# Sums read behind later splits in an expert stage, and one weight chunk in eight of some blocks multiplied without a split

## The chip, the cores and the metric

The kernel runs on one core of a Trainium2 chip. The metric is the device time of one execution in microseconds (us). Five engines take part: PE (TensorE, matrix products), DVE (VectorE), ACT (ScalarE), POOL (GpSimd, hardly used here) and SP (SyncE, which issues the loads). Each works through its own queue of instructions in order; semaphores make one wait for another. PE writes its sums into PSUM, eight banks of 128 partitions x 512 floats.

## The reference

Two transformer-like blocks over 256 tokens of width 1024, all in float32. The last and longest part is a mixture of eight experts of which each token uses two:

```
logits = h @ router_w + router_b
top_val, top_idx = top_k(logits, 2);  top_w = softmax(top_val)
for e in range(8):
    out += gates[:, e] * ((silu(h @ wg[e]) * (h @ wu[e])) @ wd[e])
```

`wg` and `wu` are 1024 x 3584, `wd` is 3584 x 1024, so the experts' weights are 352 MB, and each is read once.

## The kernel before

**Products.** A float32 product is made of three fast ones: each operand is split into a high half (rounded to the fast type fp32r) and a low half (the rest), and `mm3` adds high x high, high x low and low x high into the same bank. A split (`split`, lines 373 to 376) is a cast on ACT (line 374) and a subtraction on DVE (recorded under line 339, which `tt` uses). A plain float32 product needs no split; PE's records show it as two matmul records for one.

**Weights.** A chunk is 512 rows x 512 columns (1 MiB), laid out in memory so that one load fetches it; `raw` and `fetch` (line 393) take a raw buffer and issue the load on SP's queue. `chunk` splits it in two steps of 128 x 1024 elements into buffers `hi` and `lo`. In the expert stage there are eight raw buffers (ten at first) and six `hi` and six `lo` buffers, that is, three chunks. A buffer is free again when its last reader is done: a raw one after the second subtraction, a split one after its matmuls. Buffers are given out in the order in which they came free.

**The expert stage** (`moe`). The experts are ordered by the number of their tokens. The four largest get 128 slots each, the four others (`small`) 64. `gather` collects an expert's tokens into slots by products with a selection matrix and splits them (`XH`, `XL`); for 64 slots the high and low halves share the 128 columns, so two products do for three. An expert has seven blocks (`cb`) of 512 hidden columns. A block is six chunks:

- `up`: gate chunks 0 and 4, then up chunks 0 and 4 (numbers are the first of the four 128-row tiles), summed into one bank each;
- the gate sum goes through Silu, the product with the up sum is transposed on PE and split (`hu`);
- `down`: two chunks, which add into two banks that stay for the whole expert.

**Order.** The blocks of the 128-slot experts and those of the 64-slot experts run in turn, after four 128-slot blocks at the start and before four 64-slot ones at the end. The work is written as a pipeline: after `up` of a block come `down` half 0 of the block before, `up_end` of this block, and `down` half 1 of the block before. `mids` holds four lists of work that is run behind the four chunks of the next `up`: `end` (the split of `hu`) in the first, gathers, scatters and placements of experts in the others. A scheduler orders each engine's queue from this program order and from when it reckons an operand ready; `tc.issue_after(ins)` puts what is traced in its block behind `ins` on the same engine. `last_hi` and `last_lo` are the latest cast and subtraction of a split.

Readers of sums before: Silu of the gate sum directly behind the gate chunks; for 64 slots, copies of the gate sum (line 2128) and of the up sum (line 2138), and Silu and product only after the transposes, in `end`; the multiply of the 128-slot block in `up_end`; the `hu` cast (line 2160) and its subtraction in `end`. PSUM has three banks of class `pd` and five of class `ps` here; four `ps` hold the down sums of two experts.

At the end the last block's `end` and the last two down chunks' splits come ahead of a branch (`overflow`, for experts with too many tokens; not taken with these inputs), and the last `down`, the scatter, the norm and the stores behind it.

Of the kernel before, what the change touches and what calls it, by code (L numbers as in the profile page):

```python
# [212 lines left out]
class K:  # L213
# [1784 lines left out]
            self.nc.scalar.copy(PG, p[:, :256])  # L1998


    def gather(self, x, P, a2, b2, out, part=(0, 4)):
        for k0 in part:
            with self.scope():
                p, f = self.psum(), self.med()
# [49 lines left out]
    def moe(self, x, lg, rs):  # L2054
        A, nc = self.A, self.nc
        ad = self.ada_b
# [12 lines left out]
        NE, NB = 8, 7  # L2069
        small = [r >= SMALL for r in SEQ]  # L2070
# [21 lines left out]
        def begin(e):  # L2092
            P, PG = PP[e % 4]
            if small[e]:
                X = self.take("r", 0)
                state[e] = [PG, (X,), None]
                return [lambda: self.gather_small(x, P, ad["a2"], ad["b2"], X)]
            XH, XL = self.take("r", 0), self.take("r", 0)
            state[e] = [PG, (XH, XL), None]
            out = lambda k0, f: self.split(f, XH[:, k0 * 128 : k0 * 128 + 512], XL[:, k0 * 128 : k0 * 128 + 512])  # L2100
            return [lambda k0=k0: self.gather(x, P, ad["a2"], ad["b2"], out, (k0,)) for k0 in (0, 4)]

        def up(e, cb, mids):
            XH, XL = state[e][1][0], state[e][1][-1]
            g, ps = self.med(), []
            for nm in ("moe_w_gate_2", "moe_w_up_2"):
                p = self.take("pd")
                ps.append(p)  # L2110
                for kh in (0, 4):
                    with self.scope():
                        args = (W(nm, e), kh * 128, 4, cb * 512, 512)
                        c = self.chunk(*args)
                        for k in range(4):
                            ks = slice((kh + k) * 128, (kh + k) * 128 + 128)
                            if small[e]:
                                for i in range(2):
                                    self.last_mm = self.mm(p, XH[:, ks], c[k][i], kh + k + i == 0, kh + k + i == 8, True)
                            else:  # L2120
                                self.mm3(p, XH[:, ks], XL[:, ks], c[k][0], c[k][1], kh + k == 0, kh + k == 7)
                    for f in mids.pop(0):
                        f()
                if not small[e] and nm == "moe_w_gate_2":
                    self.act(g, p, AF.Silu)
            if small[e]:
                with self.tc.issue_after(self.last_hi.ins):
                    nc.scalar.copy(g, ps[0])
            return g, p


        def up_end(e, g, pu):
            hu = self.take("r", 0)
            p = self.take("ps", 0)
            if small[e]:
                gu = self.med()
                with self.tc.issue_after(self.last_hi.ins):
                    nc.scalar.copy(gu, pu)  # L2138
                for i, a in enumerate((g, gu)):
# [3 lines left out]
                def end():  # L2143
                    with self.scope():
                        h = self.med()
                        self.act(h[:, :256], p[:, :256], AF.Silu)
                        self.tt(h[:, 256:], p[:, 256:], h[:, :256], ALU.mult)
                        v = hu[:, :512].rearrange("p (k h s) -> p k h s", k=4, h=2)
                        self.split(h[:, 256:].rearrange("p (k s) -> p k s", k=4), v[:, :, 0], v[:, :, 1])
                    self.free(p)  # L2150
                return hu, end
            with self.scope():
                h = self.med()
                self.tt(h, pu, g, ALU.mult)
                for k in range(4):
                    self.tr(p[:, k * 128 : k * 128 + 128], h[:, k * 128 : k * 128 + 128])

            def end():
                with self.tc.issue_after(self.last_hi.ins):
                    self.last_hi = nc.scalar.copy(hu[:, :512], p)  # L2160
                with self.tc.issue_after(self.last_lo.ins):
                    self.tt(hu[:, 512:], p, hu[:, :512].bitcast(F32), ALU.subtract)
                self.free(p)
            return hu, end

        def down(e, cb, hu, half):
            hh, hl = hu[:, :512], hu[:, 512:]
            if cb == half == 0:
                state[e][2] = [self.take("ps", 0), self.take("ps", 0)]
            acc = state[e][2]  # L2170
            with self.scope():
                c = self.chunk(W("moe_w_down_2", e), cb * 512, 4, half * 512, 512)
                for k in range(4):
                    ks = slice(k * 128, k * 128 + 128)
                    first, last = cb == 0 and k == 0, cb == NB - 1 and k == 3
# [3 lines left out]
                    else:  # L2179
                        self.mm3(acc[half], hh[:, ks], hl[:, ks], c[k][0], c[k][1], first, last)  # L2180
            if half:
                self.free(hu)
# [18 lines left out]
        prev, mids = None, [[] for _ in range(4)]  # L2201
        for e, cb in steps:
            with self.scope():
                gp = up(e, cb, mids)
                mids = [[] for _ in range(4)]
                if cb == NB - 1:
                    self.free(*state[e][1])
                if prev:
                    down(*prev, 0)
                hu, end = up_end(e, *gp)  # L2210
                mids[0].append(end)
            if prev:
                for i, f in zip((1, 2), down(*prev, 1) or []):
                    mids[i].append(f)
            prev = (e, cb, hu)
# [97 lines left out]
```

## Time and profile before

| what | value |
|---|---|
| time, median of 3 runs (lowest, highest) | 2152.31 us (2149.79, 2153.07) |
| profiled execution: its time, its span | 2151.22 us, 2149.4 us |
| PE busy, share of the span | 2066.2 us, 96% |
| DVE busy | 1841.5 us, 86% |
| ACT busy | 1325.3 us, 62% |
| loads of the experts' weights | 336 of 1024 KB |
| data moved, mean rate | 610.70 MB, 284 GB/s |
| mean granted TensorE clock | 0.988 of 2.4 GHz |

The span runs from the first to the last instruction. Busy PE includes matmuls that wait in its pipeline. The expert stage is about 1165 to 2130 us of the span.

### The profile page before, as it was taken

How to read it: one execution, taken by the hardware profiler on the slowest of the kernel's cores; microseconds unless marked ns; L12 is line 12 of the kernel's file. 1: busy time of each engine (PE TensorE's matmuls, PEld its weight loads, DVE VectorE, ACT ScalarE, POOL GpSimd, SP SyncE). 2: the span in 40 equal slices, each digit the busy share in tenths (PEclk: the TensorE clock that was granted, in tenths of full speed). 3: DMA queues.
4: the chain of work that ended last, by engine and by line, in shares of the span. 5: the costliest groups of instructions: out<-in, count | busy, mean ns of one | idle time of the engine just before them, and what ended most of it. 6: DMA issues, size and time to landing. Idle time of an engine off the chain costs nothing. (4 is left out here: it accounts for less than half of the span.)

```text
span 2149.4 us, 31135 instructions
## 1 busy us (share of the span) xinstructions
PE 2066.2 (96%) x11593; PEld 1706.1 (79%) x11593; DVE 1841.5 (86%) x2669; ACT 1325.3 (62%) x1857; POOL 2.1 (0%) x6
## 2 busy tenths in 40 slices
PE   6999999999999999999999999999999999999997
PEld 5987888889988878998997887777777777777765
DVE  6888985898888868888787999998998899998997
ACT  4544354454445435444765887777787778777775
POOL 0000000000000000000000000000000000000000
PEclk9999999999999999999999999999999999999997
DMA  7546767878843527885465899998999899998993
GB/s 306 192 165 214 264 219 255 298 296 303 302 160 117 150 100 262 310 342 212 139 253 188 329 400 368 356 387 321 391 343 377 348 365 377 355 383 322 386 371 140
DMA packets 99997, 610.70 MB, mean 284 GB/s; under 512 B 19156, under 2 KB 24061, under 8 KB 27773
## 3 DMA queue, kind: packets, MB, share of 16 engines
q1 hardware_dynamic: 99836, 608.64, 75.7%
q8 instruction: 92, 1.51, 0.3%
q14 instruction: 69, 0.56, 0.1%
HBM read 606.75 MB, written 3.42 MB: 284 GB/s over the span
## 5 line engine op out<-in xcount | busy, mean ns | idle before, releaser
L354 PE MATMUL pd<-k 128*128 128x512 f32 (+2 forms) x7408 | 1447.2, 349 | 37.8 <-DVE k L339 26.6
L339 DVE TENSOR_TENSOR k<-k,k 128x1024 fp32r<-128x1024 f32 (+2 forms) x1149 | 1229.8, 1112 | 184.4 <-ACT k L374 180.9
L354 PEld LDWEIGHTS pd<-k 128*128 128x128 f32 (+1 forms) x7408 | 1139.1, 190 | 269.3 <-DVE k L339 104.0
L374 ACT CAST k<-k 128x1024 fp32r<-128x1024 f32 (+2 forms) x1131 | 1039.6, 977 | 362.9 <-PE pd L354 184.6
L354 PE MATMUL ps<-k 128*128 128x512 f32 (+8 forms) x3031 | 576.2, 343 | 13.4 <-DVE k L339 3.8
L354 PEld LDWEIGHTS ps<-k 128*128 128x128 f32 (+4 forms) x3031 | 431.6, 179 | 112.1 <-DVE k L339 18.2
L348 DVE SCALAR_TENSOR_TENSOR k<-k,k 128x512 f32<-128x512 f32 (+1 forms) x257 | 188.3, 735 | 2.1 <-ACT k L351 0.2
L351 ACT ACTIVATE k<-pd 128x256 f32<-128x256 f32 (+1 forms) x125 | 57.2, 481 | 101.4 <-PE pd L354 98.5
L351 ACT ACTIVATE k<-k 128x256 f32<-128x256 f32 (+8 forms) x142 | 69.0, 500 | 79.3 <-DVE k L339 41.7
L339 DVE TENSOR_TENSOR k<-k 128x512 f32<-128x512 f32 (+13 forms) x277 | 93.6, 355 | 17.3 <-ACT k L351 12.4
L354 PEld LDWEIGHTS ps<-k,k 128*128 128x128 f32 x526 | 77.0, 199 | 12.4 <-DVE k L348 3.4
L339 DVE TENSOR_TENSOR k<-ps,k 128x512 fp32r<-128x512 f32 (+5 forms) x99 | 56.8, 579 | 24.8 <-PE ps L354 8.7
L354 PE MATMUL ps<-k,k 128*128 128x64 f32 (+3 forms) x526 | 75.0, 269 | 2.9 <-DVE k L348 2.9
L357 PE MATMUL ps<-k,k 128*128 128x128 f32 (+1 forms) x396 | 60.8, 278 | 16.7 <-DVE k L343 15.8
L357 PEld LDWEIGHTS ps<-k,k 128*128 128x128 f32 (+1 forms) x396 | 47.9, 143 | 30.5 <-DVE k L343 18.5
L339 DVE TENSOR_TENSOR k<-pd,k 128x512 f32<-128x512 f32 (+4 forms) x108 | 59.8, 568 | 12.5 <-PE pd L354 6.5
L351 ACT ACTIVATE k<-ps,k 128x128 f32<-128x128 f32 (+2 forms) x100 | 36.6, 446 | 42.8 <-DVE k L348 26.7
L348 DVE SCALAR_TENSOR_TENSOR k<-pd,k,k 128x255 f32<-128x255 f32 (+2 forms) x96 | 43.1, 474 | 4.4 <-ACT k L351 4.0
L2138 ACT COPY k<-pd 128x512 f32<-128x512 f32 x28 | 16.4, 586 | 48.2 <-PE pd L354 47.9
L345 DVE TENSOR_SCALAR k<-ps,k 128x128 f32<-128x128 f32 (+1 forms) x90 | 32.4, 405 | 10.5 <-PE ps L354 6.9
L348 DVE SCALAR_TENSOR_TENSOR k<-k 128x256 f32<-128x256 f32 (+7 forms) x121 | 36.9, 312 | 2.8 <-ACT k L351 1.1
L351 ACT ACTIVATE k<-ps 128x256 f32<-128x256 f32 (+2 forms) x30 | 12.4, 420 | 35.3 <-PE ps L354 35.3
(95 smaller groups left out, 416.1 us busy)
## 6 DMA issues: line engine op xcount, KB each, us to landing
k<-in_moe_w_up_dram SPq DMA_DIRECT2D x112, 1024.0 KB, 7.0
k<-in_moe_w_gate_dram SPq DMA_DIRECT2D x112, 1024.0 KB, 7.1
k<-in_moe_w_down_dram SPq DMA_DIRECT2D x112, 1024.0 KB, 7.2
k<-in_ada_w_dram SPq DMA_DIRECT2D x48, 1024.0 KB, 5.3
k<-in_w_in_dram SPq DMA_DIRECT2D x44, 1024.0 KB, 6.1
k<-in_w_ff_dram SPq DMA_DIRECT2D x32, 1024.0 KB, 6.0
k<-in_w_ada_dram SPq DMA_DIRECT2D x24, 1024.0 KB, 6.7
k<-in_cd_w_in_dram SPq DMA_DIRECT2D x14, 1024.0 KB, 4.9
```

The lines of the kernel that those rows point to most:

```text
L339: return self.nc.vector.tensor_tensor(o, a, b, op=op)
L345: self.nc.vector.tensor_scalar(o, a, s1, s2, op0=op0, op1=op1)
L348: self.nc.vector.scalar_tensor_tensor(o, a, s, b, op0=op0, op1=op1)
L351: return self.nc.scalar.activation(o, a, f, **kw)
L354: return self.nc.tensor.matmul(o, l, r, start=start, stop=stop, skip_group_check=skip)
L357: return self.nc.tensor.transpose(o, i, self.ident[: i.shape[0], : i.shape[0]])
L374: self.last_hi = self.nc.scalar.copy(hi, src)
L2138: nc.scalar.copy(gu, pu)
```

## The change

Four things, all in `moe`:

1. `up` only sums. `gate_out` reads the gate sum and is run behind the splits of the first down chunk of the block before; `up_out` reads the up sum and is run in the first `mids` list, behind the splits of the next block's first gate chunk; `turn` (the transposes) is in the second list; `end` is run behind the splits of this block's first down chunk, one step later than before, directly ahead of the products that need `hu`.
2. Each of these is put behind the latest cast (`last_hi`) or the latest subtraction (`last_lo`) with `issue_after`.
3. The sums of gate, up and transposes all take a `pd` bank and give it back one by one; before, the transposes took a `ps` bank.
4. For 128-slot experts and `cb` 1, 3, 5, the second gate chunk isn't split: four plain float32 matmuls with the unsplit rows `XF`, kept from the gather, stand for its twelve.

```diff
-            return [lambda k0=k0: self.gather(x, P, ad["a2"], ad["b2"], out, (k0,)) for k0 in (0, 4)]
+            return [lambda k0=k0, f=f: self.gather(x, P, ad["a2"], ad["b2"], out, (k0,), f) for k0, f in ((0, None), (4, XF))]
...
-                        c = self.chunk(*args)
+                        own = not small[e] and nm == "moe_w_gate_2" and kh and cb % 2
+                        c = self.raw(*args) if own else self.chunk(*args)
                         for k in range(4):
                             ks = slice((kh + k) * 128, (kh + k) * 128 + 128)
-                            if small[e]:
+                            if own:
+                                self.mm(p, state[e][3][:, k * 128 : k * 128 + 128], c[:, k], False, k == 3)
+                            elif small[e]:
...
-                if not small[e] and nm == "moe_w_gate_2":
-                    self.act(g, p, AF.Silu)
...
+        def gate_out(e, b):
+            b["g"] = self.take("ms", 0)
+            with self.tc.issue_after(self.last_hi.ins):
+                if small[e]:
+                    nc.scalar.copy(b["g"], b["ps"][0])
+                else:
+                    self.act(b["g"], b["ps"][0], AF.Silu)
+            self.free(b["ps"][0])
+
+        def up_out(e, b):
+            b["h"] = self.take("ms", 0)
             if small[e]:
                 with self.tc.issue_after(self.last_hi.ins):
+                    nc.scalar.copy(b["h"], b["ps"][1])
+            else:
+                with self.tc.issue_after(self.last_lo.ins):
+                    self.tt(b["h"], b["ps"][1], b["g"], ALU.mult)
+            self.free(b["ps"][1])
+
+        def turn(e, b):
+            p = b["p"] = self.take("pd", 0)
...
+        def end(e, b):
+            p, hu = b["p"], self.take("r", 0)
+            hi, lo = self.last_hi.ins, self.last_lo.ins
...
+        def down(e, cb, b, half, after=()):
...
                 c = self.chunk(W("moe_w_down_2", e), cb * 512, 4, half * 512, 512)
+                for f in after:
+                    f()
+                hh, hl = b["hu"][:, :512], b["hu"][:, 512:]
...
-                gp = up(e, cb, mids)
-                mids = [[] for _ in range(4)]
-                if cb == NB - 1:
-                    self.free(*state[e][1])
-                if prev:
-                    down(*prev, 0)
-                hu, end = up_end(e, *gp)
-                mids[0].append(end)
+                b = {"ps": up(e, cb, mids)}
+            mids = [[] for _ in range(4)]
+            if cb == NB - 1:
+                self.free(*state[e][1])
+            if prev:
+                down(*prev, 0, [lambda: end(prev[0], prev[2]), lambda: gate_out(e, b)])
+            else:
+                gate_out(e, b)
+            mids[0].append(lambda e=e, b=b: up_out(e, b))
+            mids[1].append(lambda e=e, b=b: turn(e, b))
...
         for half in range(2):
             self.presplit(W("moe_w_down_2", NE - 1), (NB - 1) * 512, 4, half * 512, 512)
+        end(prev[0], prev[2])
```

## Rows read from the trace of the kernel before

**Rows 1.** Windows, 50 us each: busy us per engine, granted clock, DMA share, GB/s.
```profile
1250.00:1300.00 50.00, 49.69 (x228) 39.69 (x226) 47.67 (x48) 40.89 (x48) 0.00 (x0) 1.00 1.00 405
...
2000.00:2050.00 50.00, 49.46 (x225) 38.56 (x225) 44.19 (x43) 37.67 (x45) 0.00 (x0) 1.00 0.98 385
sum 800.00, PE 775.84 PEld 590.20 DVE 718.88 ACT 620.37 POOL 0.00; mean PE 48.49 PEld 36.89 DVE 44.93 ACT 38.77 POOL 0.00
```

**Rows 2.** DMA view, 1250 to 2050 us: totals; one tensor's loads, median us to landing.
```profile
DMA packets 40061, 292.01 MB, mean 365 GB/s; under 512 B 4444, under 2 KB 4444, under 8 KB 4444
...
k<-in_moe_w_up_dram SPq DMA_DIRECT2D x93, 1024.0 KB, 7.1
```

**Rows 3.** Waits of SP's queue, 1250 to 2050: us in total, times, longest.
```profile
SPq L393 <- DVE k L339: 652.5, 278, 9.1
```

**Rows 4.** Waits of DVE, 1250 to 2050 us.
```profile
DVE k L339 <- ACT k L374: 68.0, 62, 6.7
DVE k L339 <- ACT k L351: 8.5, 16, 0.5
DVE k L345 <- PE ps L354: 3.1, 1, 3.1
```

**Rows 5.** Waits of ACT, 1250 to 2050 us.
```profile
ACT k L351 <- PE pd L354: 57.2, 29, 3.8
ACT k L2138 <- PE pd L354: 38.8, 20, 2.3
ACT k L351 <- PE ps L354: 37.6, 24, 3.6
ACT k L2128 <- PE pd L354: 15.2, 13, 1.7
```

**Rows 6.** Timeline of DVE in one pair: start, us, what, [idle before, releaser].
```profile
1619.97 2.36 DVE L339 TENSOR_TENSOR k<-k,k 128x1024 fp32r<-128x1024 f32 x2 [0.59 <-ACT k L374]
1622.87 0.42 DVE L339 TENSOR_TENSOR k<-ps,k 128x256 f32<-128x256 f32 x1 [0.53 <-ACT k L351]
1623.80 7.24 DVE L339 TENSOR_TENSOR k<-k,k 128x1024 fp32r<-128x1024 f32 x7 [0.51 <-ACT k L374]
1632.30 4.63 DVE L339 TENSOR_TENSOR k<-k,k 128x1024 fp32r<-128x1024 f32 x4 [1.26 <-ACT k L374]
```

**Rows 7.** Timeline of PE in the same pair.
```profile
1621.41 1.00 PE L354 MATMUL ps<-k,k 128*128 128x64 f32 x8
...
1625.07 11.34 PE L354 MATMUL pd<-k 128*128 128x512 f32 x48
...
1638.07 0.60 PE L357 MATMUL ps<-k,k 128*128 128x128 f32 x4
```

**Rows 8.** Groups by form, 1250 to 2050 us: busy us, mean ns | idle before.
```profile
L354 PE MATMUL pd<-k 128*128 128x512 f32 x2094 | 547.9, 404 | 20.9 <-DVE k L339 17.8 <-ACT k L374 2.0
...
L339 DVE TENSOR_TENSOR k<-ps,k 128x512 fp32r<-128x512 f32 x30 | 20.4, 681 | 0.4 <-ACT k L374 0.4
...
L2160 ACT CAST k<-ps 128x512 fp32r<-128x512 f32 x20 | 11.8, 591 | 4.2 <-PE ps L357 4.2
L354 PE MATMUL ps<-k 128*128 128x64 f32 x96 | 11.7, 269 | 0.0
...
L354 PE MATMUL ps<-k 128*128 128x128 f32 x64 | 9.3, 278 | 0.9 <-ACT k L351 0.9
```

**Rows 9.** Timeline of DVE, idle times over 1.5 us, 1250 to 2050: first, last of eleven.
```profile
1285.63 3.50 DVE L339 TENSOR_TENSOR k<-k,k 128x1024 fp32r<-128x1024 f32 x3 [1.87 <-ACT k L374]
...
1983.70 4.63 DVE L339 TENSOR_TENSOR k<-k,k 128x1024 fp32r<-128x1024 f32 x4 [2.63 <-ACT k L374]
```

**Rows 10.** Timeline of PE in the modulation stage, around a plain float32 product.
```profile
389.60 1.02 PE L354 MATMUL pd<-k,k 128*128 128x512 f32 x2
390.06 2.16 PE L354 MATMUL pd<-k 128*128 128x512 f32 x7
```

**Rows 11.** Windows, the stretch of 128-slot blocks only.
```profile
1200.00:1240.00 40.00, 40.00 (x199) 33.67 (x198) 35.55 (x41) 33.10 (x43) 0.00 (x0) 1.00 0.89 335
```

More of the change, by code (lines that the diff above doesn't have):

```diff
@@ L1998, in slots, with gather @@
             self.nc.scalar.copy(PG, p[:, :256])
-    def gather(self, x, P, a2, b2, out, part=(0, 4)):
+    def gather(self, x, P, a2, b2, out, part=(0, 4), kept=None):
         for k0 in part:
             with self.scope():
-                p, f = self.psum(), self.med()
+                p, f = self.psum(), self.med() if kept is None else kept
                 for k in range(4):
@@ L2098, in begin @@
             XH, XL = self.take("r", 0), self.take("r", 0)
-            state[e] = [PG, (XH, XL), None]
+            XF = self.take("md", 0)
+            state[e] = [PG, (XH, XL, XF), None, XF]
             out = lambda k0, f: self.split(f, XH[:, k0 * 128 : k0 * 128 + 512], XL[:, k0 * 128 : k0 * 128 + 512])
-            return [lambda k0=k0: self.gather(x, P, ad["a2"], ad["b2"], out, (k0,)) for k0 in (0, 4)]
+            return [lambda k0=k0, f=f: self.gather(x, P, ad["a2"], ad["b2"], out, (k0,), f) for k0, f in ((0, None), (4, XF))]
         def up(e, cb, mids):
-            XH, XL = state[e][1][0], state[e][1][-1]
-            g, ps = self.med(), []
+            XH, XL = state[e][1][0], state[e][1][-1 if small[e] else 1]
+            ps = []
             for nm in ("moe_w_gate_2", "moe_w_up_2"):
-                p = self.take("pd")
+                p = self.take("pd", 0)
                 ps.append(p)
@@ L2123, in up @@
                         f()
[L2124 to L2125 removed]
+            return ps
+        def gate_out(e, b):
[8 more added lines that the diff above has]
+            b["h"] = self.take("ms", 0)
@@ L2135, in up_end @@
             if small[e]:
[L2136 to L2139, printed above, removed]
+                for i, a in enumerate((b["g"], b["h"])):
                     for k in range(4):
                         self.mm(p[:, i * 256 + k * 64 : i * 256 + k * 64 + 64], a[:, k * 128 : k * 128 + 128], self.cst("ident2"))
-                def end():
-                    with self.scope():
-                        h = self.med()
+            else:
+                for k in range(4):
+                    self.tr(p[:, k * 128 : k * 128 + 128], b["h"][:, k * 128 : k * 128 + 128])
@@ L2146, in end @@
+            self.free(b["g"], b["h"])
+        def end(e, b):
+            p, hu = b["p"], self.take("r", 0)
+            hi, lo = self.last_hi.ins, self.last_lo.ins
+            if small[e]:
+                with self.scope():
+                    h = self.med()
+                    with self.tc.issue_after(hi):
                         self.act(h[:, :256], p[:, :256], AF.Silu)
+                    with self.tc.issue_after(lo):
                         self.tt(h[:, 256:], p[:, 256:], h[:, :256], ALU.mult)
-                        v = hu[:, :512].rearrange("p (k h s) -> p k h s", k=4, h=2)
@@ L2149, in end @@
[L2149 to L2159, printed above, removed]
+                    v = hu[:, :512].rearrange("p (k h s) -> p k h s", k=4, h=2)
@@ L2160, in end @@
+                    self.split(h[:, 256:].rearrange("p (k s) -> p k s", k=4), v[:, :, 0], v[:, :, 1])
+            else:
+                with self.tc.issue_after(hi):
                     self.last_hi = nc.scalar.copy(hu[:, :512], p)
-                with self.tc.issue_after(self.last_lo.ins):
+                with self.tc.issue_after(lo):
                     self.tt(hu[:, 512:], p, hu[:, :512].bitcast(F32), ALU.subtract)
[L2163 to L2167, printed above, removed]
+            self.free(p)
@@ L2168, in down @@
+            b["hu"] = hu
+        def down(e, cb, b, half, after=()):
             if cb == half == 0:
@@ L2181, in down @@
             if half:
-                self.free(hu)
+                self.free(b["hu"])
             if cb == NB - 1 and half:
@@ L2203, in moe @@
             with self.scope():
-                gp = up(e, cb, mids)
-                mids = [[] for _ in range(4)]
-                if cb == NB - 1:
-                    self.free(*state[e][1])
-                if prev:
-                    down(*prev, 0)
-                hu, end = up_end(e, *gp)
-                mids[0].append(end)
+                b = {"ps": up(e, cb, mids)}
[4 more added lines that the diff above has]
+                down(*prev, 0, [lambda: end(prev[0], prev[2]), lambda: gate_out(e, b)])
+            else:
+                gate_out(e, b)
+            mids[0].append(lambda e=e, b=b: up_out(e, b))
+            mids[1].append(lambda e=e, b=b: turn(e, b))
             if prev:
@@ L2214, in moe @@
                     mids[i].append(f)
-            prev = (e, cb, hu)
+            prev = (e, cb, b)
             if (e, cb) == (0, 0):
```

5 lines of the change are left out of this document (removed).

## The prediction

> **What bounds the kernel now.** I read the page first: no engine is idle for long and the end chain explains under 1% of the span, so the limit has to be read from the stage that the change touches. That is the expert stage, about 1165 to 2130 us. The windows view of its even part, 1250 to 2050 us, shows PE marked busy nearly always, DVE 718.88 of 800 us, DMA near its full share and the granted clock 1.00 (2.4 GHz) throughout [rows 1]; busy PE is not PE at its peak, so it decides nothing yet. The DMA view of the same stretch gives 292.01 MB [rows 2], which at 1.049 MB a load is 278 loads. A block (one step of the loop) takes 6 loads, so a pair of blocks, one of a 128-slot expert and one of a 64-slot expert, takes 12: there are 23.2 pairs in 800 us, **34.5 us a pair**. I use this as the unit.
>
> Then the waits. SP's loads wait for DVE, 652.5 us over 278 loads [rows 3]: a load starts when DVE's subtraction has freed a raw buffer, so data is early and DMA isn't what comes last. DVE's idle time is nearly all for ACT, 68.0 + 8.5 us of the 79.6 listed [rows 4]. ACT in turn waits for sums of PE: Silu of the gate sum and the gathers under 57.2, the copies of the 64-slot sums 38.8 and 15.2, their Silu 37.6 [rows 5]. ACT and DVE run a queue each, so the splits of the next chunks stand behind a reader of an unfinished sum. In one pair DVE loses 0.59 + 0.53 + 0.51 + 1.26 = 2.9 us that way [rows 6]. PE then lacks low halves in the 64-slot block, while in the 128-slot block it runs 48 matmuls without a gap [rows 7].
>
> **What each resource needs for a pair.** DVE: 718.88 / 23.2 = 31.0 us busy, 3.5 idle. PE: 48 matmuls last 11.34 us to the modelled end of the last one [rows 7], and one alone is given 0.404 [rows 8], so 47 starts take 10.94, 0.233 us each. 120 of them are 28.0, the 64-slot transposes 2 x 1.00, the others 0.60 [rows 7], gathers (11.7 + 9.3) / 23.2 = 0.9 [rows 8] and about 0.4 for scatters (an estimate, 16 matmuls of 0.233 for every two experts, spread over their seven pairs): 31.9. DMA: 12.58 MB; the best 50 us moved 405 GB/s, the seven stretches with a share of 0.98 or more (1250, 1400, 1500, 1650, 1750, 1850, 2000; first and last in [rows 1]) average 388. That is 31.1 to 32.4 us.
>
> **The change, part by part.**
>
> Readers behind later splits. `gate_out` now follows the two casts of the first down chunk, `up_out` those of the next block's first gate chunk, `turn` the second gate chunk on PE, `end` the first down chunk. The high and low halves have six buffers each, three chunks. Where ACT has cast down 0, its last buffer came free only once PE had passed the chunk three back, the second gate chunk: the gate sum is complete when ACT can reach its reader. For `up_out` the chunk three back is the last up chunk; the same holds. These waits go rather than move. What DVE gets back: 79.6 us, less the eleven long waits of 1.9 to 6.7 us at changes of expert, 35.5 in all (first and last in [rows 9], the longest in [rows 4]), where gathers make ACT wait for PE; the diff moves none of those. 44 us are left, 1.9 a pair. Nothing is added: same copies, same transposes. Its cover is the lead: with none, `end` costs PE the second subtraction of down 0 (4 in 4.63 us, 1.16), a cast 0.59 and a subtraction 0.68 [rows 6, 8], 2.4 us in a block, before it may start `down`. Where DVE is behind, this is the order of the same work and PE finds a full chunk afterwards; I take 0 and keep 2.4 as the bound.
>
> PSUM: `turn` takes from the three pd banks, as gate and up do. Order of freeing gives it the bank of the gate sum, and up gets the bank of the previous up; PE reaches both after the transposes that needed the same readers. I take 0. XF holds one of the three d buffers, which nothing else in this stage uses: 0.
>
> The chunk as it is. `cb` 1, 3, 5 of four experts: 12 chunks. DVE loses 24 subtractions of 1.16 us, 27.8 us; ACT as many casts. PE does 4 plain f32 matmuls for 12. The stage has none of 512 columns; the nearest rows are those of the modulation stage, two records each: 1.02 us busy by itself, or 0.82 as what is left of the 2.62 us from its start to the end of the seven ordinary ones behind it, less 7 x 0.233 and the 0.17 by which the last one's end is past its turn [rows 10]. Bounds: 0.47 (two ordinary records) and 1.02. I take 0.9, nearer the value among other matmuls: 3.6 us a chunk against 12 x 0.233 = 2.8, +0.8, in all +10 us on PE (-11 to +15), 0.4 a pair. The raw buffer is freed by PE instead of DVE, up to three chunks (8 us) later, and SP's queue holds all later loads behind it. Eight buffers turn over every 34.5 / 12 = 2.9 us and a load needs 7.1 us [rows 2], so three cover it; I take 0, at most 12 x 2 us.
>
> Sum. DVE could give back 24 pairs x 1.9 + 27.8 = 73 us. It isn't allowed to: PE needs 31.9 + 0.4 = 32.3 a pair, DMA 32.4 at 388 GB/s. With two limits at nearly the same height and few buffers between, I put the pair at **32.6 us** (an estimate between 32.4 and 34.5, near the limits because the first blocks, all of 128 slots, keep PE busy 40.00 of 40 us [rows 11]). 24 pairs x 1.9 = 46 us. The four 128-slot blocks at the start are PE's already: two chunks as they are, +1.6 us. The end: the last `end` comes behind four splits, up to +2, and four 64-slot blocks lose waits like the three small ones of [rows 6], 1.6 us in each, of which I count half, -3. Together +1; I put 0. From the profiled execution's own 2151.2 us (span 2149.4): 2105; it lies 1.1 below the median, so **2106 us**.
>
> A rule that speaks against this: the rate at 1250 us is 405 GB/s [rows 1]. The Trainium skill, DMA: Bandwidth & Descriptors, section "Where 436 GB/s comes from", holds that loads from HBM are bound by about 358 GB/s per core; by it a pair takes 35.1 us and the change can gain nothing. The trace doesn't agree (365 on average, 405 at best), but that bound is the fourth rival's reason.
>
> **The rivals.**
> 1. Forecast, 32.6 us a pair: 2106, own range 2090 to 2125. Chance 0.55.
> 2. Only some waits go: gate sums come 3.6 us later behind a plain f32 chunk, ACT stands at `gate_out`, and DVE keeps the 1.26 of that and the 0.53 of [rows 6] or their like; it wins 0.59 + 0.51 less what gathers add, 0.85 a pair x 24 = 20: 2132. For it: 0.6 lead chunk fewer. Against: no slot is free there anyway. 0.20.
> 3. DMA goes deeper: at 405 GB/s 31.1 a pair and PE near its low bound: -80, 2072. For it: 405 over 50 us; against: PE's 31.9. 0.08.
> 4. DMA is the limit already: more early loads bring no rate above the mean of 365 GB/s, the pair stays at 34.5, 2152. For it: shares of 0.93 and more; against: 405, and SP's waits for DVE. 0.07.
> 5. Slower: PE has no lead at `down`, and every one of the 24 64-slot blocks pays the 2.4 us, 58 us, against the 46 won: +12, 2164. It decides when PE arrives before `end` in over 19 of the 24 (or as many of all blocks). For it: PE lacks low halves in just these blocks; against: DVE's extra lead of 73 us. 0.08.
> 6. The change doesn't do what it says: the order on ACT stays as the scheduler had it, and only the 12 chunks count, hidden in part: about -10, 2142. 0.02.
>
> **The numbers.** Under about 0.2% (4.3 us) a measurement of this kernel can't be told from no change. Faster: rivals 1, 2, 3, 6, 0.85, less the edge of 2, 0.84; same 0.07; slower 0.09. The range leaves out 4, 5 and the edge of 3: 2072 to 2150.
>
> **What would show it.** Right: ACT's waits for PE at the Silu and at both copies near 0, DVE's waits for ACT near 35 us a stage of this length, 24 fewer subtractions of 1024 columns, DMA share 0.98 or more at 385 to 395 GB/s, a pair of 32.3 to 33 us, in 12 places eight matmul records of one chunk at 3.3 to 4.1 us. Wrong: PE waiting for the `end` subtraction at `down`; ACT waiting at `gate_out` for more than 1 us; loads waiting for PE; a share of 1.00 at 365 GB/s.

## The result, and the profile after

| | before | after |
|---|---|---|
| time, median | 2151.05 us (4 runs) | 2121.84 us (4 runs, 2120.66 to 2122.69) |
| profiled execution: time, span | 2151.22, 2149.4 us | 2121.62, 2119.7 us |
| mean granted TensorE clock | 0.988 | 0.990 |

The ratio is 0.9864, with a 95% interval of 0.9847 to 0.9881: the change saves 29 us, where 46 were forecast. The time lies inside the stated range and inside the forecast's own range (2090 to 2125), near its upper end.

Read the same views in the same order. First the windows of the expert stage after the change, columns as in [rows 1].

```profile
1250.00:1300.00 50.00, 50.00 (x237) 40.67 (x236) 44.39 (x45) 37.90 (x45) 0.00 (x0) 1.00 0.96 398
...
1550.00:1600.00 50.00, 44.96 (x211) 36.87 (x210) 46.17 (x52) 37.03 (x45) 0.00 (x0) 0.97 0.93 340
...
2000.00:2050.00 50.00, 49.84 (x238) 41.40 (x238) 48.15 (x47) 43.10 (x51) 0.00 (x0) 1.00 1.01 422
sum 800.00, PE 774.14 PEld 622.46 DVE 724.35 ACT 634.65 POOL 0.00; mean PE 48.38 PEld 38.90 DVE 45.27 ACT 39.67 POOL 0.00
```

The DMA view of the same 800 us, against [rows 2]:

```profile
DMA packets 41624, 303.37 MB, mean 379 GB/s; under 512 B 4622, under 2 KB 4622, under 8 KB 4622
...
k<-in_moe_w_down_dram SPq DMA_DIRECT2D x96, 1024.0 KB, 7.4
```

303.37 MB are 289 loads or 24.1 pairs, so a pair takes 33.2 us where [rows 2] gave 34.5; 1.3 us in each of 24 pairs is about the gain. The stretches differ, though: 422 GB/s at 2000 us, 340 at 1550 with the clock at 0.97, and that difference carries the explanation below. The waits of the same stretch after the change, against [rows 3 to 5] (engine and line, what it waited for: us in total, times, longest):

```profile
ACT k L374 <- PE pd L354: 50.6, 107, 2.1
DVE k L339 <- ACT k L374: 49.4, 55, 6.3
ACT k L351 <- PE pd L354: 33.9, 13, 3.2
ACT k L374 <- PE ps L354: 25.1, 36, 2.1
...
ACT k L1998 <- PE ps L357: 15.8, 5, 5.4
PE ps L354 <- DVE k L339: 14.6, 16, 2.4
DVE k L339 <- ACT k L351: 13.5, 10, 1.9
PE pd L354 <- DVE k L339: 9.7, 10, 2.4
```

```profile
SPq L393 <- DVE k L339: 573.3, 247, 8.7
SPq L393 <- PE pd L354: 63.3, 10, 6.8
```

ACT's waits for finished sums fall from the 148.8 us of [rows 5] to 33.9: the copies of the 64-slot sums no longer wait at all. In their place ACT waits 75.7 us at its casts (L374 for PE). That is a wait for a free split buffer: ACT is then ahead of PE, which has split chunks in hand. DVE's waits for ACT fall only from 76.5 [rows 4] to 62.9. And PE itself stands up to 2.4 us at a time for DVE.

What PE gained is seen in the waits of its weight loads (PEld) for DVE's subtractions, in the same stretch, first before the change and then after it:

```profile
PEld pd L354 <- DVE k L339: 85.5, 182, 1.1
...
PEld ps L354 <- DVE k L339: 10.7, 28, 0.6
```

```profile
PEld pd L354 <- DVE k L339: 21.8, 38, 2.8
PEld ps L354 <- DVE k L339: 21.3, 26, 2.8
```

210 waits of at most 1.1 us have become 64 of up to 2.8 us: the many short waits are gone, and some long ones have come.

**Where the time came from.** A pair is not one thing. I take the `hu` cast of each 128-slot block (28 of them, line 2160 before, 2180 after) as a mark and read the time from mark to mark. Two stretches are of use. From the 12th to the 19th mark lie seven pairs, one whole turn with a change of a 64-slot expert and one of a 128-slot expert in it. The last pair (27th to 28th mark) has no gather, no scatter and no chunk multiplied as it is; I call such a pair ordinary. The windows cut at those marks, first of the kernel before (the turn, and the last two pairs, 32.4 us each), then of the changed one (the turn, and the last pair):

```profile
1502.90:1746.60 243.70, 235.83 (x1066) 178.48 (x1066) 218.24 (x222) 188.42 (x233) 0.00 (x0) 1.00 0.94 362
1990.20:2054.90 64.70, 63.62 (x282) 47.97 (x281) 58.89 (x57) 51.33 (x61) 0.00 (x0) 1.00 0.99 385
```

```profile
1503.10:1738.80 235.70, 226.94 (x1054) 181.83 (x1053) 211.90 (x217) 185.31 (x227) 0.00 (x0) 0.99 0.96 374
...
2005.20:2035.00 29.80, 29.73 (x142) 24.76 (x141) 29.34 (x29) 26.41 (x31) 0.00 (x0) 1.00 1.01 422
```

A pair without a change of expert took 32.4 us and takes 29.8, with PE busy 29.73 and DVE 29.34 of it: PE has no idle time left, and DVE hardly any. Seven pairs at that price would be 226.8 us before and 208.6 after. The turn takes 243.7 and 235.7, so its two changes of expert add **16.9 us before and 27.1 after**. Counted so, the change wins 18.2 us a turn in ordinary pairs and gives 10.2 back at the changes of expert (2.0 of it are three chunks multiplied as they are, priced below). This is a way of counting, not a stretch measured by itself: the placing, gathering and scattering for two experts spread over the whole turn, and of its seven pairs after the change only one comes near the low price (30.6 us with an unsplit chunk), while the others take 32.2 to 36.6. The extra time also holds the work of the gathers and scatters itself. The difference, 8.0 us in seven pairs, is 27 us in 24.

What is late at a change of expert is seen in the timeline after the change, around 1360 us (start, length, what, [idle before, releaser]), and further down in two stretches of 16 matmuls of one size:

```profile
1355.72 0.38 ACT L351 ACTIVATE k<-pd 128x256 f32<-128x256 f32 x1
...
1358.16 1.41 DVE L348 SCALAR_TENSOR_TENSOR k<-ps,k 128x512 f32<-128x512 f32 x2
...
1359.48 2.35 DVE L339 TENSOR_TENSOR k<-k,k 128x1024 fp32r<-128x1024 f32 x2
1361.75 0.42 DVE L339 TENSOR_TENSOR k<-pd,k 128x256 f32<-128x256 f32 x1
...
1362.20 0.41 ACT L374 CAST k<-k 128x256 fp32r<-128x256 f32 x1 [3.45 <-DVE k L339]
...
1363.21 0.42 DVE L339 TENSOR_TENSOR k<-k,k 128x256 fp32r<-128x256 f32 x1
...
1363.69 2.93 PE L354 MATMUL pd<-k 128*128 128x512 f32 x6 [2.40 <-DVE k L339]
...
1563.50 5.54 PE L354 MATMUL ps<-k 128*128 128x512 f32 x16 [2.29 <-DVE k L339]
...
1599.78 3.92 PE L354 MATMUL ps<-k 128*128 128x512 f32 x16 [2.40 <-DVE k L339]
```

The Silu of a 64-slot `end` is done at 1356.1, but its product (1361.75) stands on DVE behind the additions of a scatter and two subtractions; ACT's cast waits 3.45 us for it with further casts queued behind, and PE stands 2.40 us until the subtraction of that same `end` (128x256, at 1363.21) is done. PE stands like that, for 2.29 or 2.40 us, six times in the stretch, at 1326.90, 1363.69, 1563.50 and 1599.78 in its first half, always at a change of a 128-slot expert and each time until the subtraction of a 64-slot `end`. At three of the six the granted clock falls to 1.2 GHz for 3.4 us: the 16 matmuls from 1563.50 take 5.54 us, those from 1599.78, at 2.4 GHz, 3.92. Before the change it does not fall in this stretch (1.00 in its windows [rows 1]).

### The profile page after: what moved, and what is told of

It is laid out like the page before. It is cut to its first block, busy times and chain, and to the rows that moved or that the text cites. A ratio compares the mean times of both kernels' runs of the same rounds, so it can differ in the third digit from the quotient of the medians.

```text
span 2119.7 us, 31109 instructions
## 1 busy us (share of the span) xinstructions
PE 2030.7 (96%) x11545; PEld 1715.0 (81%) x11545; DVE 1817.2 (86%) x2645; ACT 1312.0 (62%) x1833; POOL 2.1 (0%) x6
## 3 DMA queue, kind: packets, MB, share of 16 engines
q1 hardware_dynamic: 99836, 608.64, 75.7%
## 5 line engine op out<-in xcount | busy, mean ns | idle before, releaser
L354 PE MATMUL pd<-k 128*128 128x512 f32 (+2 forms) x7366 | 1417.4, 349 | 24.7 <-DVE k L339 15.3
L339 DVE TENSOR_TENSOR k<-k,k 128x1024 fp32r<-128x1024 f32 (+2 forms) x1125 | 1204.6, 1112 | 170.3 <-ACT k L374 160.8
L374 ACT CAST k<-k 128x1024 fp32r<-128x1024 f32 (+2 forms) x1107 | 1029.4, 974 | 463.1 <-PE pd L354 229.2
L354 PEld LDWEIGHTS pd<-k 128*128 128x128 f32 (+1 forms) x7366 | 1141.7, 189 | 214.5 <-DVE k L339 30.2
L354 PE MATMUL ps<-k 128*128 128x512 f32 (+8 forms) x3025 | 559.8, 342 | 25.3 <-DVE k L339 18.1
L339 DVE TENSOR_TENSOR k<-pd,k 128x512 f32<-128x512 f32 (+4 forms) x155 | 85.9, 564 | 27.4 <-ACT k L351 13.5
L339 DVE TENSOR_TENSOR k<-k 128x512 f32<-128x512 f32 (+13 forms) x277 | 93.5, 355 | 17.8 <-ACT k L351 12.9
L354 PEld LDWEIGHTS pd<-k,k 128*128 128x128 f32 x472 | 63.5, 193 | 16.0 <-ACT k L2137 6.5
L354 PE MATMUL pd<-k,k 128*128 128x64 f32 (+1 forms) x472 | 69.7, 288 | 5.5 <-ACT k L2137 5.1
L357 PE MATMUL ps<-k,k 128*128 128x128 f32 x302 | 47.9, 283 | 17.3 <-DVE k L343 16.3
L357 PEld LDWEIGHTS ps<-k,k 128*128 128x128 f32 x302 | 37.2, 146 | 27.4 <-DVE k L343 19.0
L351 ACT ACTIVATE k<-ps,k 128x128 f32<-128x128 f32 (+2 forms) x100 | 37.4, 448 | 33.5 <-DVE k L348 27.1
L339 DVE TENSOR_TENSOR k<-ps,k 128x512 f32<-128x512 f32 (+5 forms) x52 | 30.8, 604 | 17.9 <-PE ps L354 7.4
L357 PE MATMUL pd<-k,k 128*128 128x128 f32 (+1 forms) x222 | 36.8, 281 | 4.9 <-DVE k L1346 4.9
L357 PEld LDWEIGHTS pd<-k,k 128*128 128x128 f32 (+1 forms) x222 | 28.1, 143 | 12.5 <-DVE k L1346 5.2
```

What stands on the lines that cost most here:

```text
L339: return self.nc.vector.tensor_tensor(o, a, b, op=op)
L351: return self.nc.scalar.activation(o, a, f, **kw)
L354: return self.nc.tensor.matmul(o, l, r, start=start, stop=stop, skip_group_check=skip)
L357: return self.nc.tensor.transpose(o, i, self.ident[: i.shape[0], : i.shape[0]])
L374: self.last_hi = self.nc.scalar.copy(hi, src)
```

## The experiments

Below, "turn" is the time of the seven pairs, "last pair" the ordinary one; both are read from each run's trace at the same marks. Each ratio is to runs of the kernel before that were timed beside it (medians 2151.0 to 2151.8 us).

| kernel | us, median | ratio to before, 95% | turn | last pair | turn less 7 x last pair |
|---|---|---|---|---|---|
| before | 2151.0 | | 243.7 | 32.4 | 16.9 |
| changed | 2121.8 | 0.9864 (0.9847 to 0.9881) | 235.7 | 29.8 | 27.1 |
| order_only | 2113.8 | 0.9826 (0.9812 to 0.9839) | 234.6 | 29.9 | 25.3 |
| raw_only | 2154.1 | 1.0017 (1.0008 to 1.0026) | 244.6 | 32.4 | 17.8 |
| end_early | 2162.3 | 1.0045 (1.0031 to 1.0058) | 246.8 | 31.9 | 23.5 |
| gate_early | 2145.8 | 0.9978 (0.9969 to 0.9987) | 242.3 | 30.3 | 30.2 |
| half_loads | 2105.1 | 0.9785 (0.9770 to 0.9800) | 230.6 | 29.6 | 23.4 |
| order_half | 2093.3 | 0.9729 (0.9716 to 0.9742) | 225.0 | 29.8 | 16.4 |
| order_rows | 2114.1 | 0.9835 (0.9820 to 0.9849) | 234.6 | 29.9 | 25.3 |
| own_narrow | 2105.5 | 0.9791 (0.9778 to 0.9805) | 231.1 | 29.8 | 22.5 |
| pe_less | 2084.2 | 0.9685 (0.9671 to 0.9698) | 224.5 | 29.3 | 19.4 |
| dve_less | 2113.7 | 0.9822 (0.9809 to 0.9836) | 232.9 | 29.6 | 25.7 |
| before_pe_less | 2126.6 | 0.9890 (0.9875 to 0.9905) | 237.2 | 31.4 | 17.4 |
| pg_late | 2131.6 | 0.9912 (0.9897 to 0.9927) | 236.9 | 29.8 | 28.3 |

### The change taken apart: order_only and raw_only

```diff
-                        own = not small[e] and nm == "moe_w_gate_2" and kh and cb % 2
+                        own = False
```

> The changed kernel with every chunk split again; only the readers of sums are moved. Lead theory (the stage is PE's in 128-slot blocks and DVE's in 64-slot blocks, with three chunks of split buffers between them; the order gains where a gather met a Silu at the change of a 64-slot expert, and nothing in ordinary pairs): 2125 to 2135 us, the gain again in the two pairs at that change. Forecast's theory (DVE's idle time and its subtractions add up until PE or DMA binds): 24 subtractions come back, 27.8 us of DVE, so of the two terms 46 and 28 the order alone keeps most: 2110 to 2122, spread over all pairs.

2113.8 us, the number of the forecast's theory: without the twelve chunks the change is 8 us **better**. raw_only is the kernel before with those chunks (and `XF`) alone:

> The kernel before with the 12 unsplit chunks and the kept rows, the readers of sums where they were. Lead theory: a chunk without a split lengthens the lead by one chunk just where PE is slow, but ACT still stands at the Silu; 2140 to 2150 us. Forecast's theory: DVE is relieved of 27.8 us in a stage in which it is what PE waits for, 2125 to 2135 us. A third possibility, that PE's extra 8 us are all that shows: 2155 to 2160.

2154.1 us, nearest to the third possibility: 24 subtractions fewer on DVE bought nothing, and about 3 us were lost. So the whole gain (37 us in order_only) is that of parts 1 to 3 of the change, the moved readers with their places in the queues and the PSUM banks, and the unsplit chunks cost in both kernels. The marks say how much: the pair before the last one has such a chunk and takes 30.6 us in the changed kernel, 29.9 in order_only; in raw_only 33.1, in the kernel before 32.4. That is 0.7 us each time.

### Why the chunk costs: own_narrow

```diff
-                                self.mm(p, state[e][3][:, k * 128 : k * 128 + 128], c[:, k], False, k == 3)
+                                self.mm(p[:, :256], state[e][3][:, k * 128 : k * 128 + 128], c[:, k, :256], False, k == 3)
```

> The changed kernel, but the four products of each chunk that is multiplied as it is go over 256 of the 512 columns; its loads, the casts and subtractions that it leaves out, and all orders stay. The sums of these columns are left incomplete. On TensorE such a chunk falls from 3.43 to about 1.72 us, below the 2.77 us of a split one. Theory A, the 8 us that the chunks as they are cost (2113.8 without them, 2121.8 with) are TensorE's time, 12 x 0.66: 12 x 1.72 = 20.6 us less, so 2101, or not below 2105 if something else takes over; in any case under 2113. Rival B, they cost because the raw buffer is held by TensorE for longer, so that SP's loads come later, or because sums are read later on ScalarE: part of the holding stays, and the time lies between 2114 and 2122.

2105.5 us, 16.3 of the 20.6 us that TensorE was spared, and 8 less than with every chunk split: theory A. The orders are those of the changed kernel but for three copies on ACT and one place on DVE. The pair with the chunk now takes 28.9 us. The price can be read off the changed kernel directly. These are weight loads of consecutive plain records around 1452 us, 0.43 us apart, and what stands behind the chunk:

```profile
1451.48 0.19 PEld L354 LDWEIGHTS pd<-k 128*128 128x128 f32 x1 [0.24 <-issue]
1451.91 0.19 PEld L354 LDWEIGHTS pd<-k 128*128 128x128 f32 x1 [0.24 <-issue]
...
1455.52 0.38 ACT L351 ACTIVATE k<-pd 128x256 f32<-128x256 f32 x1 [3.22 <-PE pd L354]
1455.93 0.43 DVE L339 TENSOR_TENSOR k<-pd,k 128x256 f32<-128x256 f32 x1 [1.43 <-ACT k L351]
```

Eight records are 3.43 us, twelve fast matmuls at 0.231 on the mean are 2.77: 0.66 more, in all twelve 8 us, which is the whole difference to order_only. The waits of ACT and DVE behind the chunk are real (33.9 and 13.5 us in the list above; ACT's is 2.8 in order_only) but own_narrow shows that they cost little: with ACT's down to 14.3 us and DVE's to 0.8 it still gained less than TensorE's own time.

### Which reader's place matters: end_early and gate_early

Both are the changed kernel with one reader moved back. In end_early `end` runs behind the third chunk of the next `up`:

```diff
-                down(*prev, 0, [lambda: end(prev[0], prev[2]), lambda: gate_out(e, b)])
+                down(*prev, 0, [lambda: gate_out(e, b)])
...
+            mids[2].append(lambda e=e, b=b: end(e, b))
...
-        end(prev[0], prev[2])
```

> The changed kernel, but end (the split of the hidden block) is run one place earlier, behind the first up chunk of the next block instead of behind its first down chunk. Theory that the place of end costs: PE's six waits of about 2.3 us for DVE at the changes of experts and the three falls of the clock to 1.2 GHz (3.4 us each, 1.7 lost) go: 2105 to 2115 us. Rival (the waits are DVE's lack of time at these places, whatever the order): they move to the chunk's own low halves, 2119 to 2124. Rival (ACT now stands at end, ahead of the down splits): 2125 to 2135.

In gate_early `gate_out(e, b)` comes directly behind `up`:

```diff
+            gate_out(e, b)
             if prev:
-                down(*prev, 0, [lambda: end(prev[0], prev[2]), lambda: gate_out(e, b)])
-            else:
-                gate_out(e, b)
+                down(*prev, 0, [lambda: end(prev[0], prev[2])])
```

> The changed kernel with `gate_out` alone run directly behind `up`, ahead of the first down chunk's splits; `end`, `up_out` and `turn` stay where the change put them. Theory A, the place of `end` carries nearly all of the gain: the time stays within 8 us of 2121.8. Rival B, the wait of ScalarE for an unfinished gate sum costs as much as that for `end`: 15 us or more on top, 2137 and above.

2162.3 and 2145.8 us: 40 and 24 us lost. Either reader ahead of the splits undoes most of the 29 us or more than all of them; every theory of end_early missed, and of gate_early rival B holds. Both kernels keep the new PSUM banks of part 3, so the banks alone don't bring the gain. In the last pair the two differ: 31.9 us with `end` early, 30.3 with `gate_out` early, against 29.8. In gate_early the clock has a share too: between 1250 and 2050 us it falls to 1.2 GHz six times, in the changed kernel three times; at 1.6 us a fall (5.54 less 3.92 in the rows above) that is some 5 us, an estimate. ACT's wait for PE at its activations, 33.9 us in the changed kernel, in end_early and then in gate_early (1250 to 2050 us):

```profile
ACT k L351 <- PE pd L354: 122.0, 26, 9.6
...
DVE k L339 <- ACT k L351: 63.4, 20, 6.0
```

```profile
ACT k L351 <- PE pd L354: 75.3, 23, 5.1
DVE k L339 <- ACT k L374: 71.0, 40, 4.4
```

One reader that stands ahead of the splits is enough to bring much of the old wait back, and DVE idles behind it as in [rows 4].

### Is it the bytes? half_loads, order_half, order_rows

half_loads is the changed kernel, order_half is order_only, both with loads of half the columns:

```diff
-        self.nc.sync.dma_start(ap[:, : kt * n], w.at(r0, kt, c0, n))
+        part = kt * n // 2 if w.ap.tensor.name.startswith("in_moe_w") else kt * n
+        self.nc.sync.dma_start(ap[:, :part], w.at(r0, kt, c0, n)[:, :part])
```

> The changed kernel with each load of expert weights cut to its first half (512 KB); the second half of every chunk is whatever the buffer held, so the sums are others. Lead theory: no wait for a load stands in the stage, 2117 to 2123 us. Forecast's theory (DMA at 388 GB/s is one of the two limits, 32.4 of the 33.2 us that a pair takes): 10 to 25 us less, 2097 to 2112.

> The changed kernel with every chunk split and only the first half (512 KB) of each expert-weight load; the second half of each raw buffer keeps old data, all instructions on the other engines stay. Beside the same kernel with whole loads (2113.8). Theory A, halving the loads gave the changed kernel 17 us because the raw buffers held by TensorE made its loads late: without such chunks halving gives 8 us less or nothing, so 2105 to 2114. Rival B, loads come late at other places too, or the transfers slow other work: halving gives 12 to 20 us here too, 2094 to 2102.

They gained 17 and 20 us, and the forecast's theory of half_loads and rival B of order_half seemed to hold: whole loads cost 20 us somewhere. But with the shorter loads the scheduler had ordered ACT, DVE and PE differently in both kernels. order_rows, again made from order_only, loads half the partitions instead, and there the order on ACT, DVE and PE is that of order_only:

```diff
-        self.nc.sync.dma_start(ap[:, : kt * n], w.at(r0, kt, c0, n))
+        r = slice(0, 64 if w.ap.tensor.name.startswith("in_moe_w") else 128); self.nc.sync.dma_start(ap[r, : kt * n], w.at(r0, kt, c0, n)[r])
```

> The kernel with every chunk split (2113.8), whose expert-weight loads fetch 64 of the 128 partitions (512 KB); the other partitions keep old data. Unlike the loads cut to half their columns, this leaves every engine's order of instructions as it is. Theory A, the 20 us that half the columns gave (2093.3) came from the bytes moved, by late buffers or by disturbed engines: the same again, 2092 to 2099. Rival B, they came from another order, because the scheduler reckoned the shorter loads as ready earlier and put readers of sums and copies elsewhere: 2110 to 2115.

2114.1 us with half the bytes, 2113.8 with all of them: the bytes alone cost nothing. order_rows does not halve a load's time, though: a `down` load lands 7.4 us after its issue in order_only, 5.8 in order_rows and 4.7 in order_half (medians, 1250 to 2050 us). That shorter loads didn't bring the 20 us is read from the traces: in none of the three is an engine's idle time in this stretch ended by a load, and the transfers don't slow the other work (a subtraction of 1024 columns takes 1.222 us on the mean in order_only and 1.219 in order_half, a cast 1.052 and 1.054). So the 20 us are the order's; that order with whole loads was not run. The turn in order_rows and in order_half, columns as in [rows 1]:

```profile
1498.70:1733.30 234.60, 225.45 (x1066) 183.52 (x1065) 218.52 (x223) 191.47 (x232) 0.00 (x0) 0.99 0.87 189
```

```profile
1495.90:1720.80 224.90, 220.76 (x1065) 183.00 (x1064) 217.25 (x222) 192.73 (x232) 0.00 (x0) 1.00 0.61 197
```

PE's and DVE's work is the same in both (1066 and 1065 matmul records, 223 and 222 DVE records); the last pair is the same too, 29.9 and 29.8 us. All of the difference lies at the changes of expert, 25.3 us against 16.4. Groups by form, 1250 to 2050 us, of order_only and then of order_half, show two waits of order_only that the other order doesn't have (busy us, mean ns | idle before):

```profile
L374 ACT CAST k<-k 128x256 fp32r<-128x256 f32 x24 | 9.7, 403 | 21.3 <-DVE k L339 21.0
...
L1998 ACT CAST k<-ps 128x256 fp32r<-128x256 f32 x5 | 1.9, 375 | 14.0 <-PE ps L357 14.0
```

```profile
L374 ACT CAST k<-k 128x256 fp32r<-128x256 f32 x26 | 10.6, 406 | 0.5 <-DVE k L339 0.5
...
L1999 ACT CAST k<-ps 128x256 fp32r<-128x256 f32 x5 | 1.8, 363 | 0.0
```

The first is the cast of a 64-slot `end` (the 3.45 us in the timeline above), the second the copy of a placed expert's selection matrix. PE idles 26.8 us for DVE between 1250 and 2050 us in order_only and 12.2 in order_half (where 5.8 for ACT are added), and the clock falls three times in the one and twice in the other.

### One of these waits moved by hand: pg_late

order_only, with that second copy kept back until the casts of the next first down chunk (the `ps` bank stays taken until then):

```diff
...
+            while later:
+                PG, p = later.pop()
+                with self.tc.issue_after(self.last_hi.ins):
+                    nc.scalar.copy(PG, p[:, :256])
+                self.free(p)
...
```

> The kernel with every chunk split (2113.8), in which the copy of an expert's transposed selection matrix (line 1998, for which ScalarE waits 14.0 + 5.8 us for TensorE in six places) comes behind the two casts of the next first down chunk, in the manner of the other readers. Theory A, such a wait at a change of expert costs the end what it lasts, as the others did: some 10 to 20 us, 2094 to 2104. Rival B, TensorE has enough split chunks there, and the wait lies in its slack: within 4 us, 2110 to 2118.

2131.6 us: both theories missed, it is 18 us slower. The copy's wait is gone, and the gathers' activations wait instead:

```profile
L351 ACT ACTIVATE k<-ps,k 128x64 f32<-128x64 f32 x24 | 7.8, 415 | 14.6 <-PE ps L354 14.6
...
L351 ACT ACTIVATE k<-ps,k 128x128 f32<-128x128 f32 x8 | 3.3, 462 | 12.4 <-PE ps L354 12.4
L2143 ACT CAST k<-ps 128x256 fp32r<-128x256 f32 x5 | 1.8, 366 | 0.0
```

In order_only the first of these groups waited 0.0 us and the second 1.7. PE's longest waits for a 64-slot `end` are 3.43 us here, 2.40 in order_only, and the clock stands at 1.2 GHz for 23.9 us of the stretch, in order_only for 10.2. Whether the bank that the copy holds or the scheduler's new order brought that about, the run doesn't tell.

### Which engine is the limit: pe_less, dve_less, before_pe_less

```diff
-                        self.mm3(acc[half], hh[:, ks], hl[:, ks], c[k][0], c[k][1], first, last)
+                        self.mm(acc[half], hh[:, ks], c[k][0], first, False)
+                        self.last_mm = self.mm(acc[half], hh[:, ks], c[k][1], False, last)
```

> The changed kernel without the low-by-high products of `down` for 128-slot experts: 8 matmuls of 512 columns fewer in each 128-slot block, 8 x 0.23 = 1.85 us of TensorE a block, 32 blocks. Theory A, TensorE sets the pace in the 128-slot blocks (ScalarE waits for it before each cast there): the gain is 40 to 59 us, 2063 to 2082. Rival B, VectorE and the buffers set the pace of a pair: under 15 us, 2107 or more. Between: the limits take turns inside a pair.

2084.2 us, 37.6 us gained: between the theories, close to A. The expectation counts 32 blocks and 59 us; four 128-slot experts of seven blocks are 28, and TensorE was spared 52 us. A limit by TensorE alone would have taken 1.85 us off the last pair, and it lost 0.5; there DVE is busy 28.86 us of 29.30:

```profile
1969.60:1998.90 29.30, 29.21 (x136) 23.24 (x135) 28.86 (x29) 25.84 (x32) 0.00 (x0) 1.00 1.01 420
```

Most of the gain is at the changes of expert, 19.4 us in place of 27.1. dve_less leaves out half of each down chunk's second subtraction:

```diff
+        if self.cut:
+            src, hi, lo = src[:, :1], hi[:, :1], lo[:, :1]
         self.last_lo = self.tt(lo, src, hi.bitcast(F32), ALU.subtract)
...
+                    self.cut = k == 2 and scope != 0 and w.ap.tensor.name.startswith("in_moe_w_down")
                     lo = self.split(v[:, k : k + step], h, l)
+                    self.cut = False
```

> The changed kernel, in which the second subtraction of low halves of each `down` chunk covers one of its two tiles: about 0.57 us of VectorE fewer a chunk, 4 chunks a pair, some 1.9 to 2.3 us of 34. Low halves of the rest are left as they were. Theory A, TensorE sets the pace: a gain under 15 us, 2107 or more. Rival B, VectorE sets it: 40 us and more, 2082 or less. Between: the limits take turns inside a pair.

2113.7 us, 8 us gained: theory A. In the last pair 0.2 us is won where DVE was spared some 2: while TensorE needs 29.7 us, DVE's time is worth little. The edit of pe_less in the kernel before:

> The kernel before without the low-by-high products of `down` for 128-slot experts: the same 8 matmuls, 1.85 us, fewer in each of the 32 such blocks, 59 us in all; in the changed kernel it gave 37.6. Theory A, TensorE already set the pace of most ordinary pairs before, and VectorE's waits for ScalarE lay in its slack: a gain of 30 us or more here too, 2121 or less. Rival B, the readers of unfinished sums set the pace before, as the prediction had it, and TensorE only after the change: a gain under 20 us, 2132 or more.

2126.6 us, 24.4 of the same 52: between. The last pair falls from 32.4 to 31.4, by about half of what TensorE was spared. That speaks for a pace that, before the change, was set by neither engine alone but by both in turn, through the readers. In pe_less, dve_less and before_pe_less the scheduler's order changed as well, so their split between ordinary pair and change of expert is less certain than the sums.

## Why the prediction came out as it did

**Right, and of about the right size, in an ordinary pair.** The prediction said that readers of unfinished sums cost DVE 2.9 us a pair [rows 6], 1.9 on the mean, and that the change takes these waits away. In an ordinary pair 2.6 us went (32.4 to 29.8), and end_early and gate_early bring 2.1 and 0.5 of it back. These waits were not the whole limit, though: in before_pe_less the same pair gained 1.0 us from TensorE alone. Rival 6, that the scheduler keeps the old order, is excluded by the waits of the copies; rival 4, that DMA goes no higher than 365 GB/s, by the 422 of the last pair.

**The step that failed: "the diff moves none of those".** It spoke of the long waits at changes of expert [rows 9]. I set them aside as a constant and spread 1.9 us evenly over 24 pairs. The changes of expert are no constant: 16.9 us a turn before, 27.1 after, 25.3 without the unsplit chunks. With `end` directly ahead of `down`, PE stands for `end` twice a turn, 4.7 us, and the clock falls once; at 1.6 us a fall (5.54 less 3.92) that is by estimate 6.3 of the 10.2 us by which a turn's extra time grew. My reading is that a scatter's additions or a gather on DVE find no slack there any more, with PE at its limit in an ordinary pair and DVE close to it. That the order at these places costs 8.9 us a turn is shown (order_half against order_rows, same work on PE and DVE). That PE's longest waits there are for `end` is read from the trace; what moving `end` at these places alone would give back was not isolated.

**The limits were too high, the changes of expert too cheap.** I capped the pair at 32.3 us by PE and 32.4 by DMA. The last pair runs in 29.8. PE's 32.3 held 1.3 us of gathers and scatters and 0.4 of unsplit chunks that an ordinary pair doesn't have; the 30.6 that are left are still 0.8 too many, in part because the transposes' two groups were taken at their modelled 1.00 us (from the start of such a group to the next matmul it is 0.81 us in the changed kernel, 1454.48 to 1455.29). The DMA cap took the mean of stretches that other engines had limited, 388 GB/s, for a limit of its own: the last pair moves 422. The Trainium skill, DMA: Bandwidth & Descriptors, section "Where 436 GB/s comes from", has about 358 GB/s per core bind such loads. The trace disagrees here more clearly than before the change (422 GB/s in the window from 2000 us). In order_rows, halving the bytes changed the time by 0.3 us. That a pair of 32.6 came near the mean of 33.2 is in part luck, two errors of opposite sign: the ordinary pair is shorter than I had it, and the changes of expert, 1.3 us of PE a pair in my sum, cost more: the mean lies 3.4 us above the ordinary pair, of which the unsplit chunks are 0.3.

**The chunk as it is.** The price on PE was taken as 0.8 us a chunk, 10 in all, and is 0.66, 8 in all. That the 27.8 us of subtractions would be worth nothing under PE's limit was right; but the sum put the chunks' cost under the cap, where it vanished, and it doesn't: without them the kernel is 8 us faster. Of the 17 us between the gain forecast and the gain measured this is 8; the rest, by subtraction and not by a run, I put down to the changes of expert. The Trainium skill, FP8 and Floating Point Precision, section "TensorE Precision Notes", counts four passes for a plain float32 product, by estimate 4 x 0.231 = 0.92 us of 512 columns; the trace has 0.86. The raw buffers' later release, taken at 0, shows as SP's 63.3 us of waits for PE (47.2 in own_narrow). TensorE's own 8 us already are the whole difference to order_only, so these waits cost nothing that can be seen.

**The rivals.** Rival 5's mechanism, PE standing at `down` for `end`, is there at the price given as its bound (2.4 us; measured 2.29 to 2.40), but at changes of expert and not in the 64-slot blocks throughout. Rival 2's, ACT standing at a reader behind a plain float32 chunk, is there too (3.22 us at 1455.52), not at `gate_out` but at the Silu of a 64-slot `end`, and nearly free. Rival 3 came nearest to the limit of an ordinary pair, 29.8 us being even below its 31.1, and missed the changes of expert. Of the signs named for a right forecast, the copies' waits and the chunk's 3.43 us came; DVE's waits for ACT (62.9 us, not 35; 35.3 in order_only), the DMA share (0.96 over a turn, not 0.98) and the pair (33.2 us, not 33.0 or less) did not. Two signs of a wrong one came: PE waiting for `end` at `down`, and loads waiting for PE.

**A faster version.** order_only, 2113.8 us, leaves nothing out and beats both kernels. order_half suggests that the same work, in another order at the changes of expert, could take some 20 us less: whole loads in its turn would need 392 GB/s (an estimate, 84 loads of 1.049 MB in 224.9 us), and the last pair moves 422. An order that does so with whole loads was not found here.

## What to carry to other kernels

Divide a stage into its steady part and its changes before pricing anything: a mean over both hides that an edit can speed one and slow the other. Move a reader of a sum behind the splits that PE needs first, all of the readers, since one left ahead brings the wait back; and once the engines have little idle time left, look at the irregular work that used to fall into their idle time. Where a scheduler makes the order, an experiment that changes an instruction's size can change the order too: compare the orders, and find a form of the experiment that leaves them alone.

## What was not expected of the hardware

Half the bytes over half the partitions (order_rows) keep the DMA engines marked busy for 0.87 of the turn at 189 GB/s, half the bytes over half the columns (order_half) for 0.61 at 197, and whole loads for 0.97 at 376 in order_only. A busy share near 1 is thus no proof of a rate that can't be passed: the same loads ran at 422 GB/s with a share of 1.01 where the engines asked for them.
